# Squares written into an empty slot, weight sums moved around a layer norm, and an idle product in the query projection

## The chip, the cores and the metric

The kernel runs on one core of one Trainium2 chip, as one program. The metric is the device time of one execution in microseconds (us). The core's engines are TensorE (PE in the profile, with its weight loads as PEld), VectorE (DVE), ScalarE (ACT), GpSimd (POOL) and SyncE (SP). SP does no arithmetic here: it issues transfers (DMA), one behind the other in its own order. POOL and ACT issue some transfers too.

## The reference

One layer of an encoder for 512 tokens of width 1024, in float32:

```
n = rms_norm(x);  proj = n @ w_in                  # xa 512 | zu 1024 | zv 1024 | gate_a 1024 | gate_b 1024
ya = s5_branch(xa)                                 # two linear recurrences over the tokens, gelu, a GLU
zv = layer_norm(gelu(zv), ln_g, ln_b)
yb = gelu(zu) * (w_s mixes zv within chunks of 128 tokens, per head, + bias)
h = x + (sigmoid(gate_a) * (ya @ w_proj_a) + sigmoid(gate_b) * (yb @ w_proj_b)) @ w_out
h = h + attention(rms_norm(h) @ w_q, memory keys, memory values) @ w_xo      # 4 heads, 256 memory tokens
h = h + (silu(hn @ w_gate) * (hn @ w_up)) @ w_down                           # hn = rms_norm(h), inner width 2816
out = rms_norm(h)
```

The layer norm of zv is over 1024 columns of a token: the mean is taken off, the squares of what is left are summed, and the row is scaled with the root of their mean.

## The kernel before, in words

**Products.** Every product of float32 matrices is made of three: each operand is split into a high part, rounded to a shorter float, and the low rest (`split`: ACT casts `whi`, line 85, DVE subtracts for `wlo`, line 86), and high times high, high times low and low times high are added up in a PSUM bank. A weight block of 512 KB comes by a DMA that SP issues (`wraw`, three buffers), is split two blocks ahead of its use, and feeds 24 products of 512 columns, or of 256 columns where a product is cut in halves.

**Sums of weights.** w_proj_b, w_q, the gates and w_down are multiplied by a scheme of seven half-size products in place of eight. It needs sums of weight blocks. For w_proj_b and w_q these are made in DRAM: SP copies one block into a scratch tensor (`bsum`, `qsum`; line 272), and POOL adds another onto it by a DMA that accumulates (line 273). `plan_sums` gives each of these jobs a place: the number of the weight block at which SP's copy is issued, and how many blocks later POOL's sum follows. Two of w_proj_b's sums are sums of sums, so SP's copy of such a one waits until POOL's sum has landed.

**The stage of the norm.** From about 90 to 170 us PE does the zv columns and then the gate_a columns of w_in (tiles `pt`, `pf`, 512 columns a product). In between it does small work of the S5 branch: it turns tiles (`pw`, 128 columns), ACT copies them out (`wt`, line 855), and PE multiplies with the copies (`pz`, 64 columns), whose results ACT copies to `zh`. The PSUM banks of `pw` and `pz` are three in turn. The norm of zv runs beside this, for four tiles of 128 tokens (`layer_norm`): ACT takes off the mean (`zt<-zt,nm`, line 996), squares two halves and sums them (`sum_sq`, line 483: the squares themselves, `sq`, are not used, only their sum `ss`), DVE makes the mean (`ms`), POOL the root (`r`, line 1001), and ACT scales (`zt<-zt,r`, line 1002). The tile for the unused squares comes from the pool with the tag `ev`, two buffers. The gate_a tiles that ACT makes (`gas`, line 1035) come from the same pool; SP stores them to DRAM (`gad`, line 1036), and a buffer is free again when its store has landed.

**The query projection.** w_q is multiplied as 14 half-size products of 24 matrix products each, all of 256 columns (`query_product`, line 1098), with the scores of the first heads between them. The operands are parts of `hn` and sums of them (`hse`, `hsd`).

**The units.** The gate and up columns follow the same scheme from about 574 to 794 us (`pf`, `px`, `pv`, `pq`). Once, before the last columns of the gate, `between` issues one idle product (line 1560): weights from the first block of `fn_hi`, 512 columns of its fifth block, into a bank that nobody reads. `fn` and `hn` are tiles of the same two slots at the same addresses.

**What sets the order.** A scheduler orders the instructions of each engine by its own estimate of times; `in_order` pins an instruction to its place in the program. Small side work is handed out by `later` and `tick` between weight blocks.

Of the kernel before, what the change touches and what calls it, by code (L numbers as in the profile page):

```python
# [17 lines left out]
P = 128  # L18
# [34 lines left out]
def hybrid_layer_kernel(  # L53
# [26 lines left out]
    def aux(name, shape=(P, 512)):  # L80
        return pa.tile(list(shape), F32, tag="aux", name=name)
# [175 lines left out]
    def plan_sums(places):  # L257


        jobs = []  # L260
        for w, sums in ((w_proj_b, bsum), (w_q, qsum)):
            for q, first, more in ((5, (0, 0), (0, 1)), (7, (0, 1), (1, 1)), (6, None, (1, 1)), (4, None, (1, 0))):
                for n in range(2):
                    jobs.append((sums[q, n], sums[q + (-1 if q == 6 else 2), n] if first is None else
                                 pair_block(w, *first, n), pair_block(w, *more, n)))
        for q, i, jc, more in ((5, 0, 0, lambda c: down_block(0, 1, c)), (7, 0, 1, lambda c: down_block(1, 1, c)),
                               (6, 1, 1, lambda c: down_sum(5, c)), (4, 1, 0, lambda c: down_sum(6, c))):
            for c in range(CHUNKS):
                jobs.append((down_sum(q, c), down_block(i, jc, c), more(c)))
        assert len(jobs) == len(places)  # L270
        for (dst, src, more), (j, step) in zip(jobs, places):
            plan[j][1].append((0, lambda d=dst, x=src: tc.keep_in_program_order(nc.sync.dma_start(d, x))))
            plan[j + step][1].append((0, lambda d=dst, x=more: nc.gpsimd.dma_start(d, x, accum_op=ALU.add)))  # L273
# [41 lines left out]
    for i in range(4):  # L315
# [4 lines left out]
    plan_down(w_down, lambda q, c: down_tokens[0](q, c), down_plan)  # L320
    plan_units(UNITS, down_plan)

    plan_sums([(j, 3) for j in (5, 8, 11, 13, 15, 17, 20, 22, 25, 28, 32)] + [(51 + 2 * i, 2) for i in range(4)] +
              [(67 + 3 * i, 3) for i in range(3)] + [(85 + 3 * i, 3) for i in range(3)] +
              [(95 + 2 * i, 2) for i in range(3)] + [(122 + 4 * i, 4) for i in range(16)])
    used_w = [0]

    def next_w(*key):
# [122 lines left out]
    def tick(us=5.2):  # L451

        side["now"] += us / 5.2
        run_due()
        side["credit"] = min(side["credit"] + us * side["rate"], us)
        while side["credit"] > 0.0 and side["gen"] is not None:
            try:
                used = next(side["gen"])
            except StopIteration:
                side["gen"] = None  # L460
                return
            if used is None:
                side["credit"] = 0.0
                return
            side["credit"] -= used
# [12 lines left out]
    mhalf = cp.tile([P, 9], F32, name="mhalf")[:, 0:1]  # L478
    nc.vector.memset(mhalf, -0.5)

    def sum_sq(dst, src):
        sq = np_.tile([P, 512], F32, tag="ev", name="sq", bufs=2)
        act = nc.scalar.activation(sq[:, :src.shape[-1]], src, AF.Square, accum_out=dst)
        if pinned[0]:
            in_order(act)
# [501 lines left out]
    tokm(w_in, OFF_V + 512, xn, KD, zv_evac(1))  # L987


    def layer_norm(t):  # L990

        nm, ss, ms, r = (np_.tile([P, 1 + (k == "ss")], F32, tag=k, name=k, bufs=2) for k in ("nm", "ss", "ms", "r"))
        nc.vector.tensor_tensor(nm, zsum[:, t, 0:1], zsum[:, t, 1:2], ALU.add)
        nc.vector.tensor_scalar(nm, nm, -1.0 / GW, None, ALU.mult)
        z = zt[:, t, :]
        nc.scalar.activation(z, z, AF.Identity, bias=nm)
        for i in range(2):
            sum_sq(ss[:, i:i + 1], z[:, HALF[i]])
        nc.vector.tensor_tensor(ms, ss[:, 0:1], ss[:, 1:2], ALU.add)
        nc.vector.tensor_scalar(ms, ms, 1.0 / GW, EPS, ALU.mult, ALU.add)  # L1000
        nc.gpsimd.tensor_tensor(r, ms, mhalf, ALU.pow)
        nc.scalar.activation(z, z, AF.Copy, scale=r)
# [86 lines left out]
    def product(ps, u, q, start, ops):  # L1089

        hi, lo = next_w(u[0], u[1], q)
        for j in range(2):
            cs = slice(j * P, (j + 1) * P)
            for k in range(4):
                a = (hi[:, k, cs], lo[:, k, cs])
                b = (ops[q][0][:, k, :], ops[q][1][:, k, :])
                for i, (x, y) in enumerate(((0, 0), (0, 1), (1, 0))):
                    nc.tensor.matmul(ps[:, j, :], a[x], b[y], start=start and j == k == i == 0,  # L1098
                                     stop=k == 3 and i == 2, skip_group_check=True)
        tick(2.7)  # L1100

    def unit_bank(name):
        return bank(name).rearrange("p (j t) -> p j t", j=2)

    def seed(x):
        v = unit_bank("qv")
        nc.scalar.copy(v, x)
        return v
# [291 lines left out]
    qx, qq_ = unit_bank("qx"), None  # L1400
    query_product(qx, 0, 1, True)
    qv = seed(qx)
    qq_ = unit_bank("qq")
    query_product(qq_, 0, 5, True)
    query_product(qv, 0, 2)
# [149 lines left out]
        feat_block(ps, ws[i], fn, KD, 4, ts, ts is T0)  # L1555
        tick(2.7)

    def between():

        in_order(nc.tensor.matmul(aux("idle"), ops[1][0][:, 0, 0:P], fn_hi[:, 4, :], start=True, stop=True))  # L1560

    gate_part(0, T0)
    begun = unit_start(UNITS[0])
    gate_part(1, T0)
    unit_second(UNITS[0], begun[1])
    between()
    for i in range(2):
        gate_part(i, T1)
    for j in range(2):
# [219 lines left out]
```

## Time and profile before

| | |
|---|---|
| three runs | 902.88, 905.46, 905.97 us (median 905.46) |
| the profiled execution | 903.66 us |
| its span, first to last instruction | 901.9 us |
| mean granted TensorE clock | 0.997 |
| PE busy | 887.9 us (98%) |
| DVE, ACT, POOL busy | 642.8, 484.8, 108.2 us |

The profile is of one execution. An engine's busy time is that of its instructions; an idle time is put down to what ended it. Products of PE overlap: one of 512 columns lasts about 0.40 us and the next one starts about 0.23 us after it, so the distance of starts tells the rate, and the length does not. `x6` behind a row counts merged instructions. SPq and POOLq are issues of transfers.

### The profile page before, as it was taken

The numbers are of one execution on the slowest core, as the hardware profiler recorded it, in microseconds if no ns is written. First come the engines' busy times: TensorE is split into PE (matmuls) and PEld (weight loads), VectorE is DVE, ScalarE is ACT, GpSimd is POOL, SyncE is SP. The second block draws the span as 40 slices with busy tenths as digits, with TensorE's granted clock in tenths as the row PEclk, the third lists the DMA queues.
The fourth block names the chain that finished last, engine by engine and source line by source line (L and its number), as shares of the span: only waits on it lengthen the run. The fifth ranks groups of instructions, "written<-read, shape, count | busy, mean of one in ns | idle before, by whom it ended". The sixth has DMA issues, their size and how long they took to land.

```text
span 901.9 us, 14886 instructions
## 1 busy us (share of the span) xinstructions
PE 887.9 (98%) x5787; PEld 793.5 (88%) x5787; DVE 642.8 (71%) x1048; ACT 484.8 (54%) x714; POOL 108.2 (12%) x165
## 2 busy tenths in 40 slices
PE   9999989999999999999999999999999999999996
PEld 6888878888889998889889978999999999988875
DVE  5696651889857457858856845776778777899875
ACT  5533966344388344447655634655554554665664
POOL 1004410100022201001100101101121111000010
PEclk9999999999999999999999999999999999999999
DMA  7566763566523689854979748429799999356672
GB/s 249 163 156 182 168 164 114 162 140 153 147 89 95 161 264 308 265 157 144 257 239 257 200 117 210 140 50 231 167 263 224 215 226 256 99 161 202 203 234 99
DMA packets 118408, 165.36 MB, mean 183 GB/s; under 512 B 11825, under 2 KB 84161, under 8 KB 118210
## 3 DMA queue, kind: packets, MB, share of 16 engines
q1 hardware_dynamic: 97474, 135.74, 47.2%
q0 software_dynamic: 20576, 28.15, 19.8%
q8 instruction: 45, 0.74, 0.3%
q10 hardware_dynamic: 288, 0.52, 0.2%
q14 instruction: 25, 0.20, 0.1%
HBM read 157.61 MB, written 46.63 MB: 226 GB/s over the span
## 4 chain that ended last, share of the span: by engine, by line
PE 84%; ACT 0%; DVE 0%; issue 0%; POOLq 0%; ACTq 0%
PE pf L356 21%; PE pt L356 12%; PE px L1098 12%; PE dx L356 6%; PE pq L1098 6%; PE dq L356 3%; PE pv L1098 3%; PE bx L1098 3%; PE qx L1098 2%; PE dv L356 2%; PE bq L1098 1%; PE qq L1098 1%; PE qv L1098 1%; PE psc L356 1%; PE po L356 1%; PE ptr L517 1%
## 5 line engine op out<-in xcount | busy, mean ns | idle before, releaser
L86 DVE TENSOR_TENSOR wlo<-wraw,whi 128x1024 fp32r<-128x1024 f32 (+1 forms) x145 | 172.2, 1188 | 100.3 <-ACT whi L85 92.8
L85 ACT CAST whi<-wraw 128x1024 fp32r<-128x1024 f32 (+1 forms) x145 | 148.2, 1024 | 153.5 <-PE pf L356 45.3
L356 PE MATMUL pf<-xn,whi 128*128 128x512 f32 x448 | 140.4, 394 | 0.0
L356 PEld LDWEIGHTS pf<-xn,whi 128*128 128x128 f32 x448 | 83.6, 189 | 16.8
L356 PE MATMUL pf<-xn,wlo 128*128 128x512 f32 x224 | 87.6, 391 | 0.0
L1098 PE MATMUL px<-fn,whi 128*128 128x256 f32 x480 | 83.3, 277 | 0.0
L1098 PEld LDWEIGHTS px<-fn,whi 128*128 128x128 f32 x480 | 72.5, 188 | 0.2
L85 ACT CAST whi<-b 128x1024 fp32r<-128x1024 f32 x40 | 42.2, 1054 | 50.7 <-PE px L1098 27.7
L86 DVE TENSOR_TENSOR wlo<-b,whi 128x1024 fp32r<-128x1024 f32 x40 | 48.9, 1222 | 27.9 <-ACT whi L85 27.9
L1098 PE MATMUL px<-fn,wlo 128*128 128x256 f32 x240 | 66.4, 277 | 0.0
L1098 PE MATMUL pq<-s,whi 128*128 128x256 f32 x320 | 55.0, 276 | 0.0
L356 PE MATMUL dx<-whi,s 128*128 128x512 f32 x170 | 53.6, 391 | 0.4 <-DVE h L1714 0.4
L85 ACT CAST whi<-t 128x1024 fp32r<-128x1024 f32 x30 | 31.6, 1054 | 35.3 <-PE pv L1098 12.4
L86 DVE TENSOR_TENSOR wlo<-t,whi 128x1024 fp32r<-128x1024 f32 x30 | 36.7, 1224 | 19.4 <-ACT whi L85 19.4
L356 PEld LDWEIGHTS pf<-xn,wlo 128*128 128x128 f32 x224 | 42.2, 188 | 8.9
L1098 PEld LDWEIGHTS pq<-s,whi 128*128 128x128 f32 x320 | 48.1, 188 | 0.0
L1098 PEld LDWEIGHTS px<-fn,wlo 128*128 128x128 f32 x240 | 45.1, 188 | 0.0
L1098 PE MATMUL pq<-s,wlo 128*128 128x256 f32 x160 | 44.2, 276 | 0.0
L356 PE MATMUL pt<-whi,xn 128*128 128x512 f32 x128 | 42.9, 406 | 0.1
L356 PEld LDWEIGHTS dx<-whi,s 128*128 128x128 f32 x170 | 31.8, 188 | 7.4 <-issue 0.8
L356 PE MATMUL dx<-wlo,s 128*128 128x512 f32 x85 | 33.1, 391 | 0.0
L273 POOL DMA_DIRECT2D dsum<-in_w_down_dram x12 | 13.3, 1110 | 144.3 <-DMA dsum<-in_w_down_dram 144.3
(456 smaller groups left out, 2308.3 us busy)
## 6 DMA issues: line engine op xcount, KB each, us to landing
wraw<-in_w_in_dram SPq DMA_DIRECT2D x36, 512.0 KB, 4.3
dsum<-in_w_down_dram SPq DMA_DIRECT2D x20, 512.0 KB, 6.0
wraw<-dsum SPq DMA_DIRECT2D x20, 512.0 KB, 4.5
b<-in_w_gate_dram SPq DMA_DIRECT2D x15, 512.0 KB, 5.1
b<-in_w_up_dram SPq DMA_DIRECT2D x15, 512.0 KB, 5.9
wraw<-in_w_down_dram SPq DMA_DIRECT2D x15, 512.0 KB, 4.4
dsum<-in_w_down_dram POOLq DMA_DIRECT2D x10, 512.0 KB, 8.1
dsum<-dsum POOLq DMA_DIRECT2D x10, 512.0 KB, 8.0
```

The lines of the kernel that those rows point to most:

```text
L85: hi = nc.scalar.copy(dst_hi, src)
L86: lo = nc.vector.tensor_tensor(dst_lo, src, dst_hi.bitcast(F32), ALU.subtract)
L273: plan[j + step][1].append((0, lambda d=dst, x=more: nc.gpsimd.dma_start(d, x, accum_op=ALU.add)))
L356: m = nc.tensor.matmul(ps, a[x], b[y], start=start and i == 0, stop=stop and i == 2, skip_group_check=free)
L517: nc.tensor.transpose(ps[:, j, :], src[:, k * P:(k + 1) * P], ident)
L1098: nc.tensor.matmul(ps[:, j, :], a[x], b[y], start=start and j == k == i == 0, stop=k == 3 and i == 2, skip_group_check=True)
```

## The change

Three edits. First, `layer_norm` hands `sum_sq` a place for the squares: slot A, a quarter of which was a token tile of x each, and which is empty between the input norm and `sv`. It has a part for every one of the eight squares, so none waits for a buffer of `ev`. Second, the places of w_proj_b's eight sums: three are at blocks 5, 7 and 9, and the other five at 16 to 24, where before the eight stood at 5, 8, 11, 13, 15, 17, 20 and 22; the first three of w_q go from 25, 28, 32 to 26, 28, 32. Third, the idle product becomes a helper, `idle_product`, with the old use before the gate's last columns and a new one in w_q, behind the first of the 14 products and the copy that follows it.

```
-    plan_sums([(j, 3) for j in (5, 8, 11, 13, 15, 17, 20, 22, 25, 28, 32)] + [(51 + 2 * i, 2) for i in range(4)] +
-              [(67 + 3 * i, 3) for i in range(3)] + [(85 + 3 * i, 3) for i in range(3)] +
-              [(95 + 2 * i, 2) for i in range(3)] + [(122 + 4 * i, 4) for i in range(16)])
+    plan_sums([(5, 3), (7, 3), (9, 2)] + [(j, 3) for j in (16, 18, 20, 22, 24, 26, 28, 32)] +
+              [(51 + 2 * i, 2) for i in range(4)] + [(67 + 3 * i, 3) for i in range(3)] +
+              [(85 + 3 * i, 3) for i in range(3)] + [(95 + 2 * i, 2) for i in range(3)] +
+              [(122 + 4 * i, 4) for i in range(16)])
...
-    def sum_sq(dst, src):
-        sq = np_.tile([P, 512], F32, tag="ev", name="sq", bufs=2)
+    def sum_sq(dst, src, sq=None):
+        if sq is None:
+            sq = np_.tile([P, 512], F32, tag="ev", name="sq", bufs=2)
         act = nc.scalar.activation(sq[:, :src.shape[-1]], src, AF.Square, accum_out=dst)
...
+    squares = slot("A", (P, NT, GW), F32, "squares")
+
     def layer_norm(t):
...
         for i in range(2):
-            sum_sq(ss[:, i:i + 1], z[:, HALF[i]])
+            sum_sq(ss[:, i:i + 1], z[:, HALF[i]], squares[:, t, HALF[i]])
...
+    def idle_product(x, y):
+
+        in_order(nc.tensor.matmul(aux("idle"), x[:, 0, 0:P], y[:, 4, :], start=True, stop=True))
...
     qv = seed(qx)
+    idle_product(hops[1][0], hn_hi)
     qq_ = unit_bank("qq")
...
-    def between():
-
-        in_order(nc.tensor.matmul(aux("idle"), ops[1][0][:, 0, 0:P], fn_hi[:, 4, :], start=True, stop=True))
-
...
-    between()
+    idle_product(ops[1][0], fn_hi)
```

The scheduler answers the new buffers and places with another order in the norm's stage. The line numbers of the changed kernel are 2 to 5 higher.

ACT in the norm's stage before, from the scaling of the first two tiles on. `sq,ss` are the squares with their sums, `gas` the gate tiles:

```order
L1002 ACTIVATE zt<-zt,r 128x1024 x2
...
L855 COPY wt<-pw 128x512 x2
L1035 ACT_TABLE_LOAD
L1035 ACTIVATE gas<-pf_1091 128x512
L85 CAST whi<-wraw 128x1024
L1035 ACTIVATE gas<-pf_1092 128x512
L866 COPY zh<-pz 64x8x64
L867 COPY zh<-pz 64x8x64
L483 ACTIVATE sq,ss<-zt 128x512
L855 COPY wt<-pw 128x512 x2
L483 ACTIVATE sq,ss<-zt 128x512 x3
L855 COPY wt<-pw 128x512
L1002 ACTIVATE zt<-zt,r 128x1024
```

ACT there now:

```order
L485 ACTIVATE squares,ss<-zt 128x512 x2
...
L1006 ACTIVATE zt<-zt,r 128x1024 x2
L1000 ACTIVATE zt<-zt,nm 128x1024
L1006 ACTIVATE zt<-zt,r 128x1024
...
L857 COPY wt<-pw 128x512
L485 ACTIVATE squares,ss<-zt 128x512 x2
L857 COPY wt<-pw 128x512
L1039 ACT_TABLE_LOAD
L1039 ACTIVATE gas<-pf_1093 128x512
L85 CAST whi<-wraw 128x1024
L1039 ACTIVATE gas<-pf_1094 128x512
L1006 ACTIVATE zt<-zt,r 128x1024
```

The squares of the last two tiles, which stood behind the first two gate tiles, stand before them, and so does the third scaling. On PE the `pz` group that uses these two `wt` copies has moved back: 24 products of 512 columns stood between it and the `pw` group before it, now 34.

POOL from the first root of the norm on, before (`bsum_82`, `_79`, `_80`, `_76`, `_75` are sums of w_proj_b; `ss` memsets belong to the S5 branch):

```order
L1001 TENSOR_TENSOR r<-ms,mhalf 128x1
L273 DMA bsum_82<-in_w_proj_b_dram 512x1x256
L1001 TENSOR_TENSOR r<-ms,mhalf 128x1
L273 DMA bsum_79<-in_w_proj_b_dram 512x1x256
L273 DMA bsum_80<-in_w_proj_b_dram 512x1x256
L1001 TENSOR_TENSOR r<-ms,mhalf 128x1 x2
...
L273 DMA bsum_76<-in_w_proj_b_dram 512x1x256
L273 DMA bsum_75<-in_w_proj_b_dram 512x1x256
```

And now:

```order
L1005 TENSOR_TENSOR r<-ms,mhalf 128x1 x4
...
L273 DMA bsum_82<-in_w_proj_b_dram 512x1x256
...
L273 DMA bsum_79<-in_w_proj_b_dram 512x1x256
L273 DMA bsum_75<-in_w_proj_b_dram 512x1x256
L273 DMA bsum_80<-in_w_proj_b_dram 512x1x256
L273 DMA bsum_76<-in_w_proj_b_dram 512x1x256
```

The four roots stand in a row, and the sums that stood between them come behind. Two more (`bsum_78`, `bsum_81`) have moved ahead of the first memsets and stores of the S5 kernels. On SP the copy for `bsum_78` now stands between a weight load and the loads of `rowci`, and the copy `bsum_75<-bsum_79`, which waits for POOL's `bsum_79`, between weight loads and gate stores.

PE in w_q, where the first product (`qx`) ends and the second (`qq`) begins, now; before, the row with `idle` is not there:

```order
L1102 MATMUL qx<-hn,whi 128x256 x2
L1102 MATMUL qx<-hn,wlo 128x256
L1108 MATMUL idle<-hn 128x512
L1102 MATMUL qq<-hse,whi 128x256 x2
L1102 MATMUL qq<-hse,wlo 128x256
```

One product of 512 columns has come in between.

## The prediction

> **What bounds the kernel now.** I read the page first, then the cores, the waits, the timelines of the stage that shows waits, and counts of products in stretches.
>
> ```profile
> PE 887.9 (98%) x5787; PEld 793.5 (88%) x5787; DVE 642.8 (71%) x1048; ACT 484.8 (54%) x714; POOL 108.2 (12%) x165
> PE 84%; ACT 0%; DVE 0%; issue 0%; POOLq 0%; ACTq 0%
> core 0: 901.9 us, clock 0.997
> ```
>
> PE is busy for 98% of the span and is nearly the whole chain that ended last, so a gain needs PE idle time, clock, or the spacing of PE's products. The profiled execution took 903.66 us; its span leaves 1.8 us outside, which the change does not touch. The waits from 90 to 150 us hold most of the idle time that PE has after its start; here PE's two, from its timeline (start, length, and in brackets the idle time before with what ended it), and ACT's two longest:
>
> ```profile
> 127.28 0.66 PE L854 MATMUL pw<-ident,wsx 128*128 128x128 f32 x4 [1.48 <-ACT wt L855]
> 134.57 1.76 PE L861 MATMUL pz<-u,wt 128*128 128x64 f32 x8 [1.87 <-ACT wt L855]
> ...
> ACT sq L483 <- DMA gad<-gas: 4.0, 1, 4.0
> ACT zt L1002 <- POOL r L1001: 2.9, 1, 2.9
> ```
>
> PE waits twice for ACT's copies `wt`. ACT is late for two reasons: a square waits for the store of a gate tile, and a scaling waits for POOL's root `r`. The timelines of ACT, POOL and SP show the places:
>
> ```profile
> 125.90 0.63 ACT L483 ACTIVATE sq<-zt 128x512 f32<-128x512 f32 x1 [4.00 <-DMA gad<-gas]
> 126.64 1.07 ACT L855 COPY wt<-pw 128x512 f32<-128x512 f32 x2
> 132.90 1.15 ACT L1002 ACTIVATE zt<-zt,r 128x1024 f32<-128x1024 f32 x1 [2.87 <-POOL r L1001]
> ...
> 130.82 1.15 POOL L273 DMA_DIRECT2D bsum<-in_w_proj_b_dram  x1 [13.05 <-DVE ms L1000]
> 131.47 2.64 POOL L1001 TENSOR_TENSOR r<-ms,mhalf 128x1 f32<-128x1 f32 x2
> ...
> 118.22 1.77 SPq L1036 DMA_DIRECT2D gad<-gas  x2
> ```
>
> The square shares a pool of two buffers with the gate tiles `gas`, whose stores were issued at 118.22; it starts at 125.90, and the `wt` copies stand behind it in ACT's order. The last roots stand behind a weight sum on POOL. Stretches of equal kind (us, PE busy with its count, clock, DMA) price the rest:
>
> ```profile
> 125.00:127.30 2.30, 0.82 (x7) 0.50 (x5) 0.00 (x0) 1.38 (x4) 0.00 (x0) 1.00 1.07 379
> 132.40:134.60 2.20, 0.33 (x3) 0.03 (x1) 1.27 (x2) 1.70 (x3) 1.71 (x2) 1.00 0.92 89
> 134.60:138.30 3.70, 3.70 (x16) 3.42 (x17) 1.22 (x1) 3.69 (x4) 0.00 (x0) 0.54 0.65 104
> 464.26:498.18 33.92, 33.92 (x291) 1.00 0.88 257
> 583.26:586.79 3.53, 3.53 (x32) 1.00 0.93 242
> 587.39:621.39 34.00, 34.00 (x303) 1.00 0.46 124
> 788.59:794.24 5.65, 5.65 (x49) 1.00 0.19 49
> ```
>
> Right after the second idle the clock is 0.54 over 3.70 us, so 1.70 us of clock is lost. In the last four rows all products but one have 256 columns, and the count holds two or three that run over from before. So w_q's stretch does 288 products at 117.8 ns, and the units' stretch 300 at 113.3 ns: two spacings of the same product, neither with an idle gap. Both last: once begun, each holds for the whole stretch.
>
> **The change part by part.** *Squares into the empty slot.* The four pairs are the same instructions on the same shapes; only the buffer differs, and with it the wait for the gate's store. Removed: PE's 1.48 us behind ACT's 4.00. *Sums around the norm.* Three of w_proj_b's eight sums go ahead of the norm, five behind it, so that POOL has the four roots in a row. Removed: ACT's 2.87 and with it PE's 1.87.
>
> ```profile
> 122.47 0.62 PE L356 MATMUL pf<-xn,whi 128*128 128x512 f32 x2
> 123.15 0.62 PE L356 MATMUL pf<-xn,whi 128*128 128x512 f32 x2
> 117.79 1.89 PE L861 MATMUL pz<-u,wt 128*128 128x64 f32 x16
> 115.21 1.07 ACT L855 COPY wt<-pw 128x512 f32<-128x512 f32 x2
> 109.90 2.18 ACT L1002 ACTIVATE zt<-zt,r 128x1024 f32<-128x1024 f32 x2
> 102.96 0.61 ACT L483 ACTIVATE sq<-zt 128x512 f32<-128x512 f32 x1
> ```
>
> Neither wait can move to the next link for free, since ACT now has more to do early. Ahead of the second `wt` copy that ended at 116.28 stand two more pairs of squares (about 0.61 each, 2.5 together) and one more scaling (half of 2.18): 3.5 us, so it ends near 119.8. PE wants it at 117.79 now; in the new order it does ten more products of 512 columns first (three in 123.15 - 122.47 = 0.68, so 2.3 us), and wants it near 120.1. About 0.3 us of cover is left, and the next two groups of PE stand equally close behind ACT. No row shows ACT this full with that order, so I bound what remains of the waits: nothing, or 2.0 us (ACT late by the 2.5 us of squares at one place, less some cover); I take 0.4, near the low end, because PE was moved by about what ACT gained in work. Upwards, the idle counts begin at the end of a 0.40 us product whose follower would start after 0.23, so each wait may be worth 0.17 more. Clock: 1.70 us, gone if the idle that precedes it is gone.
>
> A rule of the Trainium skill, "TensorE: Matmul & The Clock Gate", section "HAM oscillation — how this bites in real kernels", asks for an idle gap of more than about 3.4 us before the clock falls. Here a gap of 1.87 us, with 1.48 us of idle some 5 us earlier, was followed by the fall: the trace does not agree. Were the fall not due to these gaps, it would stay, which is a rival below.
>
> The three early sums go into 47 to 75 us. The second stands ahead of the loads of `rowci`, which PE turns at 58.09:
>
> ```profile
> 58.09 1.18 PE L652 MATMUL pbc<-ident,rowci 32*128 32x32 f32 x16
> 47.13 0.37 SPq L137 DMA_DIRECT2D wraw<-in_w_in_dram  x1
> 50.71 1.24 SPq L648 DMA_DIRECT2D rowci<-in_s_c_im_dram  x2
> bsum<-in_w_proj_b_dram SPq DMA_DIRECT2D x3, 512.0 KB, 7.3
> rowci<-in_s_c_im_dram SPq DMA_DIRECT2D x2, 128.0 KB, 3.4
> ```
>
> The copy, issued behind the load of 47.13 near 47.6, lands near 54.9 by its row, and `rowci`, 3.4 us from its second issue near 51.3, near 54.7, or, if it must follow the copy in full, at 58.3. So 0 to 0.2 us; I take 0.
>
> *Idle product.* It costs its own place. The same helper stands once before the units' first gate columns:
>
> ```profile
> 586.68 0.28 PE L1098 MATMUL pv<-fn,wlo 128*128 128x256 f32 x1
> 586.79 0.40 PE L1560 MATMUL idle<-fn 128*128 128x512 f32 x1
> 587.03 0.86 PE L356 MATMUL pf<-fn,s 128*128 128x256 f32 x6
> ```
>
> That is 587.03 - 586.79 = 0.24 us. Ahead of it 30 products took 3.53 us (117.7 ns), behind it 300 took 34.00 (113.3). The new one has the same operands by address (both tiles are the same slot), the same kind of product ahead (117.8) and 256-column products behind. If it does the same, 288 products gain 4.4 ns each, 1.28 us; less 0.24 and some 0.03 for the first products: 1.0 us gained. If it does nothing it costs 0.24; these are the ends, and I take the gain.
>
> [...]
>
> Sum: 903.66 - 1.48 - 1.87 - 1.70 + 0.40 - 1.00 = 898.0. The runs of before are 902.88, 905.46 and 905.97, so the profile is 1.8 below their median. I do not add that: what varies between runs may well be these waits on transfers. The upper end of the range holds it.
>
> **The rivals.** (1) *The idle product does not switch the spacing.* For it: the twelve products of 512 columns that end at 788.59 leave the 48 behind them at 117.7. Against: those take weights and columns from different tiles, and 586.79 is the closer match. 903.66 - 4.65 + 0.24 = 899.3. (2) *The clock falls all the same.* For it: the clock's window need not begin with the gap. Against: the fall begins at the very end of the second gap, and the rows before and behind it have a clock of 1.00. 898.0 + 1.7 = 899.7. (3) *ACT becomes the bound of the norm's stage*, with the squares on top of a full engine:
>
> ```profile
> 100.00:122.00 22.00, 22.00 (x135) 19.44 (x134) 15.06 (x19) 21.67 (x28) 5.12 (x5) 1.00 0.59 130
> ```
>
> It is busy for 21.67 of 22 us. Against: it then stands idle for 4 us, so the work fits. With the whole 2.0 us left: 899.6; if such a wait brings the clock down too, 901.3. (4) *Spacing is a matter of chance in time, not of operands*, so that any shift undoes it: w_q stays slow and pays 0.24, and the units' 1,700 products from 587 to 780 fall back by 4.4 ns, 7.5 us: 899.3 + 7.5 = 906.8, slower. It decides where the units' stretch begins. Against: the rows around 587 hang on what PE does just before, which is unchanged. (5) *SP stands still.* Its copies for the last sums wait for POOL's sums to land, and weight loads and gate stores queue behind them:
>
> ```profile
> bsum<-in_w_proj_b_dram POOLq DMA_DIRECT2D x7, 512.0 KB, 6.6
> bsum<-bsum SPq DMA_DIRECT2D x4, 512.0 KB, 5.3
> SPq L137 <- DVE wlo L86: 48.5, 8, 14.4
> ```
>
> Copy and sum take 11.9 us. Weight loads already wait 48.5 us for free buffers, and three blocks of 24 products (5.4 us each) lie ahead, so a hold hurts from about 16.3 - 3.7 (a load's landing) = 12.6 us on. Were POOL itself 10 us late there, two holds would cost some 9 each: 916, slower. Against: no cast of ACT waits for a load in these rows.
>
> **How the numbers follow.** Forecast 0.57 (897 to 899.5 by its own bounds), (1) 0.17, (2) 0.07, (3) 0.11, (4) 0.05, (5) 0.03. A measurement of this kernel tells 0.3% (2.7 us) from no change. Forecast to (3) lie 3.5 us or more under the median, of which I leave 0.06 for runs near the edge: faster 0.86; same 0.09, from that and half of (4) and (5) mild; slower 0.05. The range 895.4 to 902.0 takes in (1) to (3), both 0.17 above, and most of the runs' own spread.
>
> **What would show it.** Right: no PE wait for `wt` between 90 and 150, no square behind a gate's store, four roots in a row on POOL, clock 1.00 there; an idle product of some 0.24 us at about 459, and some 300 products in the 34 us behind it. Wrong: a wait of PE for ACT near 120 to 128; 288 products behind the idle one; a gap at `pbc` near 58; a cast that waits for a load near 165 to 200; the units at 117.8.

## The result, and the profile after

The changed kernel takes 898.43 us (median of 16 runs, 896.11 to 903.09), the kernel before 902.93 us (16 runs, the three shown above among them). The ratio is 0.9948 with a 95% interval of 0.9932 to 0.9963: 4.7 us faster, between 3.3 and 6.1. The forecast was 898.0 us, the range 895.4 to 902.0. One run of a later kernel (e10_act), 1271.64 us at a granted clock of 0.65, is in the slow state and stays out of that kernel's ratio.

The profiled execution of the changed kernel took 901.19 us, with a span of 899.4: it is the second longest of the sixteen, and that has to be kept in mind when the two profiles are compared. The page of the changed kernel:

```profile
span 899.4 us, 14887 instructions
PE 885.8 (98%) x5788; PEld 791.0 (88%) x5788; DVE 642.8 (71%) x1048; ACT 484.8 (54%) x714; POOL 106.8 (12%) x165
```

Its stretches of the norm's stage (us, then busy time and count of PE, PEld, DVE, ACT, POOL, then the granted clock, DMA share, GB/s), at the same times as those shown of before:

```profile
100.00:122.00 22.00, 22.00 (x128) 19.18 (x127) 14.03 (x22) 21.87 (x35) 2.62 (x3) 1.00 0.21 62
125.00:127.30 2.30, 2.30 (x12) 1.91 (x11) 2.23 (x3) 2.27 (x4) 0.00 (x0) 1.00 0.77 244
132.40:134.60 2.20, 2.20 (x22) 2.20 (x22) 1.67 (x2) 1.78 (x3) 0.00 (x0) 1.00 0.49 170
134.60:138.30 3.70, 3.70 (x20) 3.07 (x19) 0.00 (x0) 3.48 (x5) 0.00 (x0) 1.00 0.20 73
```

Where PE was busy for 0.82 of 2.30 us and for 0.33 of 2.20, it is now busy throughout, and the clock behind is 1.00 where it was 0.54. ACT does more in the same 22 us (21.87 busy, 35 instructions for 28). The places themselves, from the timelines of POOL, ACT and PE:

```profile
97.08 0.56 POOL L1005 TENSOR_TENSOR r<-ms,mhalf 128x1 f32<-128x1 f32 x1
120.80 0.55 POOL L1005 TENSOR_TENSOR r<-ms,mhalf 128x1 f32<-128x1 f32 x1 [8.04 <-ACT wt L857]
120.11 0.58 ACT L857 COPY wt<-pw 128x512 f32<-128x512 f32 x1
121.00 1.89 PE L863 MATMUL pz<-u,wt 128*128 128x64 f32 x16
```

The first and the last of the four roots wait for no weight sum. The copy `wt` that the prediction worried about ends at 120.69, and PE wants it at 121.00: 0.31 us of cover, where 0.3 was worked out.

How much that is worth shows best from two fixed points of PE that lie on either side of the stage: the first product `pbc` and the first `psv`. Of before, then of the changed kernel:

```profile
31.25 1.94 PE L652 MATMUL pbc<-ident,rowbr 32*128 32x32 f32 x16
...
171.32 0.94 PE L1051 MATMUL psv<-wsx,zt 128*128 128x128 f32 x7
```

```profile
32.19 1.94 PE L654 MATMUL pbc<-ident,rowbr 32*128 32x32 f32 x16
...
166.82 3.73 PE L1055 MATMUL psv<-wsx,zt 128*128 128x128 f32 x32
```

From 140.07 us to 134.63: 5.44 us less. The same can be done for the rest: from `psv` to w_q's first product 290.10 before and 292.06 after, from there to the first product `po` behind the scores (w_q's stage) 45.81 and 46.18. So this execution gained 5.44 in the norm's stage, and lost 0.94 ahead of it, 1.96 behind it and 0.37 in w_q. The idle product's stage, which was to gain 1.0, came out longer. Its rows:

```profile
461.58 0.28 PE L1102 MATMUL qx<-hn,wlo 128*128 128x256 f32 x1
461.70 0.40 PE L1108 MATMUL idle<-hn 128*128 128x512 f32 x1
461.94 0.40 PE L1102 MATMUL qq<-hse,whi 128*128 128x256 f32 x2
```

and the stretches ahead of it and behind it:

```profile
458.88:461.70 2.82, 2.82 (x25) 2.82 (x24) 2.35 (x4) 1.71 (x3) 0.00 (x0) 1.00 0.66 224
462.29:488.00 25.71, 25.71 (x229) 25.70 (x228) 12.92 (x14) 12.14 (x16) 2.27 (x2) 1.00 0.78 231
```

The idle product does what it was to do: 24 products in 2.82 us ahead of it (117.5 ns, one runs over from before) and some 227 in 25.71 behind it (113.3 ns). It cost 0.24 us. Yet the 1.0 us did not arrive in this execution: two distances of `qq` near 489 us were together 0.3 us too long, PE waited 0.23 us for `prob` near 496 us, and behind that wait the products ran at 117.8 ns to the end of the stage, where in every other profile they end it at 113.3. Some lines of PE's list of waits over the span:

```profile
PE pt L357 <- DVE wlo L86: 1.3, 2, 0.8
PE pt L357 <- ACT whi L85: 0.8, 2, 0.5
PE ppt L1387 <- DVE prob L1378: 0.2, 1, 0.2
```

Whether these waits belong to the change or to this execution is what the experiments had to say first.

### The profile page after: what moved, and what is told of

Same layout as the page of the kernel before. It is cut to its first block, busy times and chain, and to the rows that moved or that the text cites. A ratio compares the mean times of both kernels' runs of the same rounds, so it can differ in the third digit from the quotient of the medians.

```text
span 899.4 us, 14887 instructions
## 1 busy us (share of the span) xinstructions
PE 885.8 (98%) x5788; PEld 791.0 (88%) x5788; DVE 642.8 (71%) x1048; ACT 484.8 (54%) x714; POOL 106.8 (12%) x165
## 4 chain that ended last, share of the span: by engine, by line
PE 94%; DMA 3%; ACT 1%; DVE 1%; SPq 1%; issue 0%; POOL 0%; POOLq 0%; ACTq 0%
PE pf L357 26%; PE pt L357 16%; PE px L1102 12%; PE dx L357 6%; PE pq L1102 6%; PE dq L357 3%; PE pv L1102 3%; PE qx L1102 2%; PE bx L1102 2%; PE dv L357 2%; PE pz L863 2%; PE pk L806 2%; PE qq L1102 1%; PE bq L1102 1%; DMA slab<-in_s_log_step_dram 1%; PE psc L357 1%
```

## The experiments

The theory after the result (T1): the norm's part is the whole gain, and the 1.2 us of w_q's spacing are given back in waits. Against it stand the prediction's own sum (T2, 1.0 us net for the idle product) and chance (T3, the spacing in w_q has nothing to do with the idle product). The first four kernels take the change apart.

**Without the new idle product (e1_norm).**

```
-    idle_product(hops[1][0], hn_hi)
```

> The change without the new idle product in w_q: squares in slot A and the moved sums are kept. Theory T1 (the norm's part is the whole gain; the idle product switches the spacing, but w_q's attention steps give its 1.2 us back in waits and spacing): no PE wait for wt from 90 to 150 us, clock 1.00 there, PE's starts behind the norm 5.4 us earlier than in the kernel before (1.65 + 2.04 between starts, 1.70 of clock); time as the changed kernel, within 0.3 us of it, about 4.5 below before. Theory T2 (the prediction: the idle product is worth 1.0 net): about 1.0 us above the changed kernel, 3.5 below before. Theory T3 (w_q's first stretch at 113.3 ns in the changed kernel came from the shift in time and not from the idle product): here too 113.3 ns from the second product of w_q on, and 0.24 us below the changed kernel.

Measured: 898.23 us (10 runs), ratio 0.9953 (0.9935 to 0.9971). From `pbc` to `psv` 134.62 us, as in the changed kernel; w_q at 117.8 ns from its first product on, its stage 45.81 us as before. T1's number, and T3 falls: without the product, this execution has no switch.

**The idle product alone (e2_idle).** The kernel before, with

```
     qv = seed(qx)
+    idle_product(hops[1][0], hn_hi)
```

> The kernel before with the idle product in w_q alone. The norm's stage stays as before: PE idle near 127 and 134 us and clock near 0.5 behind it. T1: 256-column products of w_q at 117.8 ns ahead of the idle product and at 113.3 ns behind it, for some 260 products (1.2 us earlier by the end of that stretch), and most of it given back before the heads' last products, by waits for prob or by later products that fall to 117.8 ns: time within 0.3 us of before. T2: 1.0 us below before, the start of w_o's first product (pt behind the heads) 1.0 us earlier against w_q's first. T3: no switch, 0.24 us above before.

Measured: 903.13 us (12 runs), ratio 1.0004 (0.9985 to 1.0023). No gain in time. But its trace does not bear T1 out: the spacing switches behind the idle product, and w_q's stage is 44.96 us, 0.85 shorter than 45.81, with nearly nothing given back. So the single execution shows a gain of 0.85 and the times of twelve show none, with a standard error of some 0.6 us, so that they do not exclude it. One more thing is seen here: the norm's stage took 139.09 us, not 140.07, though its program is that of before.

**The squares alone (e3_squares).** The changed kernel with the old table of places and without the new idle product.

> Squares in slot A alone, with the old places of w_proj_b's sums and no new idle product. Two weight sums still stand between the roots on POOL, but the scheduler now puts all squares and the third and fourth scalings ahead of the second gate tile. If each PE gap has its own cause as the prediction reads it: the first gap (1.65 us between starts) is gone, and what is left is at most one gap of 0 to 2 us where ACT scales behind a sum on POOL. Clock: if the fall needs the gap of 1.87 us or one like it, it goes with that gap and stays with it; if it comes at this place anyway (a rival), 1.7 us of clock loss stays with no gap ahead of it. Time between 1.6 us (gap left, clock lost) and 5.4 us (neither) below before; I expect the latter, since the scalings that waited now have a gate tile and a cast less ahead.

Measured: 903.04 us (10 runs), ratio 1.0004 (0.9987 to 1.0021). The stage is cured (134.63 us from `pbc` to `psv`, no gap, no fall of the clock), and the time is that of before. From 90 to 150 us ACT waits neither for a store nor for a root, although two weight sums still stand between POOL's roots: the last root starts at 119.00 us there, where the kernel before has its last two from 131.47 us on. So the squares' edit alone takes away both waits. What was gained is lost between `psv` and w_q: 295.59 us, where the others have 289.4 to 292.1. PE's waits from 150 to 460 us, of which the kernel before has none:

```profile
PE pf L356 <- ACT ya_hi L85: 1.1, 1, 1.1
PE bq L1101 <- ACT s L85: 0.8, 1, 0.8
PE pt L356 <- DVE wlo L86: 0.5, 1, 0.5
PE bq L1101 <- DVE s L86: 0.3, 1, 0.3
PE bx L1101 <- ACT u L1119: 0.2, 1, 0.2
```

The scheduler had answered the new buffers with another order not only in the norm's stage but also in w_proj_b, where PE now does a group of `bq` products earlier and waits for their sums, and at `ya_hi`. These waits are 2.9 us of the 5.5; the rest was not taken apart. My expectation of 5.4 us was right for the stage and wrong for the kernel.

**The moved sums alone (e4_sums).** The changed kernel with the squares back in the pool of the gate tiles, and without the new idle product:

```
-            sum_sq(ss[:, i:i + 1], z[:, HALF[i]], squares[:, t, HALF[i]])
+            sum_sq(ss[:, i:i + 1], z[:, HALF[i]])
```

> The moved sums alone, with the squares still in the pool of the gate tiles and no new idle product. The four roots stand in a row, so no scaling waits for POOL and the gap of 1.87 us is gone (2.04 between starts). Two pairs of squares still stand behind the gate tiles, so a square waits some 4 us for the store of one, and PE some 1.5 us behind it. Clock: if it takes both gaps, or the longer one, the clock stays at 1.00 and the time is 3.7 us below before; if one gap of 1.5 us is enough, the clock falls some microseconds behind it and the time is 2.0 below before.

Measured: 899.94 us (10 runs), ratio 0.9965 (0.9946 to 0.9984). From `pbc` to `psv` 136.58 us, 3.49 less than before (expected 3.7). The square still waits for a gate's store, but 1.5 us and not 4.0: the store is issued at 118.26, where it was 118.22, and the square starts at 121.15, where it was 125.90. The sums that were moved away had also been in this store's way, it seems: from 90 to 150 us the transfers took 0.35 of the DMA engines here, and 0.65 in the kernel before (r3_before). ACT's and PE's waits there:

```profile
ACT sq L485 <- DMA gad<-gas: 1.5, 1, 1.5
ACT zt L1004 <- POOL r L1003: 1.0, 2, 0.8
...
PE pw L856 <- ACT zh L869: 1.0, 1, 1.0
PE pz L863 <- ACT wt L857: 0.5, 1, 0.5
```

Two gaps of 1.0 and 0.5 us, and the clock stays at 1.00.

Two of these kernels, e3_squares and e4_sums, had entered w_q at 113.3 ns without an idle product there. That made a new theory, T4: the spacing at that place is set anew in every execution, and the idle product gains only where it finds 117.8. The next two kernels are repetitions, to part the kernels by more runs and to see a second execution of each.

**The changed kernel again (r1_after).** No edit.

> The changed kernel once more, beside the same kernel without its idle product in w_q, to part the two by more runs and to see a second profiled execution. The kernels tried so far without that idle product entered w_q at 117.8 ns in two executions and at 113.3 ns in two others, so a new theory T4: without it the spacing there is set by chance (where PE's last wait ahead of w_q falls), and the idle product gains only where chance has set 117.8. T4: w_q's first product at either spacing, 113.3 ns behind the idle product in any case; time within 0.5 us of the kernel without it (gain 1.0 in about half the executions, loss 0.24 in the others: 0.4 below on average). T2 (the prediction): 1.0 us below the kernel without it.

**The change without the new idle product again (r2_norm).** No edit against e1_norm.

> The change without the idle product in w_q once more, unchanged from the first time, to see a second profiled execution of the same instructions. T4 (the spacing is set anew in each execution): w_q may run at 113.3 ns here, where it ran at 117.8 the first time, with the last wait of PE ahead of w_q at another product. The rival (the spacing belongs to the program, its operands and order): w_q at 117.8 ns again, all 311 products of it. Time as before, 898.2 within 0.7.

Measured: 896.50 us (5 runs, ratio 0.9931, 0.9918 to 0.9943) with the idle product and 897.79 (5 runs, 0.9942, 0.9930 to 0.9954) without. In these runs, taken side by side, the means are 897.01 and 898.03: 1.0 us less with the idle product, with a standard error of 0.5. The earlier runs, taken at different times, say 0.3 more (898.68 in 16 runs, 898.38 in 10; standard error 0.55), and all runs thrown together 0.0 (898.28 in 21 runs, 898.26 in 15; 0.45). The times therefore do not decide between T2's 1.0 and T4's 0.4; the traces have to. The stretches of w_q, of r1_after and then of r2_norm:

```profile
458.73:491.00 32.27, 32.27 (x287) 32.27 (x286) 19.46 (x28) 18.69 (x30) 3.35 (x3) 1.00 0.90 262
```

```profile
455.73:492.40 36.67, 36.67 (x313) 36.66 (x312) 22.31 (x31) 20.67 (x32) 3.40 (x3) 1.00 0.85 252
```

285 products in 32.27 us (113.3 ns) against 311 in 36.67 (117.8). The stage took 44.80 us in r1_after and 45.81 in r2_norm: in this execution the idle product gained 1.01 us, as forecast, and no wait took it back. So T1 falls as well: the waits in the first profile of the changed kernel were that execution's. r2_norm came to w_q at 117.8 again, which fits T4 and its rival alike; that the same order can come to it at 113.3 is shown by e6_idle256 below, whose PE has the same order up to that place.

**No idle product at all (e5_no_idle).** Against e1_norm:

```
-    idle_product(ops[1][0], fn_hi)
```

> The change without any idle product: neither the new one in w_q nor the old one ahead of the gate's last columns. If that product is what sets the spacing: the gate's last columns and the units go on at 117.8 ns as the products ahead of it, 1,701 products of 256 columns at 4.5 ns more, 7.6 us less its own 0.24: 905.6, 7.3 above the kernel with it. If the spacing of the units is set by something else (chance, or the products that follow): 113.3 ns there, and 0.2 us below, 898.0.

**The old idle product with 256 columns (e6_idle256).** Against e1_norm:

```
-        in_order(nc.tensor.matmul(aux("idle"), x[:, 0, 0:P], y[:, 4, :], start=True, stop=True))
+        in_order(nc.tensor.matmul(aux("idle")[:, 0:256], x[:, 0, 0:P], y[:, 4, 0:256], start=True, stop=True))
```

> The change without the idle product in w_q, and with the old idle product ahead of the gate's last columns cut from 512 to 256 columns, same weights and place. If what switches the spacing is one product of another length between products of 256 columns: no switch here, the units at 117.8 ns, 7.5 us above the kernel with 512 columns, 905.7. If any added product shifts the spacing (by its operands, or by its time alone): 113.3 ns behind it, and 0.1 us below, 898.1.

Measured: 905.12 us (10 runs, ratio 1.0017, 1.0003 to 1.0032) and 905.31 us (10 runs, 1.0029, 1.0013 to 1.0045), where 905.6 and 905.7 were expected. The units, first of e5_no_idle, then of e6_idle256, and in the second also w_q:

```profile
582.00:616.00 34.00, 34.00 (x291) 34.00 (x290) 24.48 (x24) 17.54 (x20) 1.68 (x2) 1.00 0.45 123
```

```profile
456.20:491.00 34.80, 34.80 (x310) 34.80 (x308) 21.21 (x29) 20.48 (x32) 3.02 (x3) 1.00 0.88 258
576.46:610.00 33.54, 33.54 (x287) 33.54 (x286) 23.45 (x23) 17.50 (x21) 2.07 (x2) 1.00 0.44 118
```

288 products in 34.00 us and 284 in 33.54 are 118 ns each: without the 512 columns the units stay at the wider spacing for all of their 1,701 products, and from the first `px` to the first `dx` they take 213.54 and 213.65 us, where every other kernel takes 206.21 (but for e7_pauses below, which has pauses there). The idle product is the cause of the narrower spacing, and it is its length that counts: the same weights and the same place with 256 columns do nothing. The first row of e6_idle256 shows w_q at 113.3 ns (307 products in 34.80) with no idle product there.

**Which gaps make the clock fall (e7_pauses).** Against e1_norm, ahead of each unit from the second on, with the units' products held in their written order:

```
+    def pause(n):
+        g = aux("pause")
+        in_order(nc.tensor.matmul(g, ops[1][0][:, 0, 0:P], fn_hi[:, 4, :], start=True, stop=True))
+        for _ in range(n):
+            in_order(nc.scalar.copy(g, g))
+        in_order(nc.tensor.matmul(g, ops[1][0][:, 0, 0:P], fn_hi[:, 4, :], start=True, stop=True))
...
+        if i:
+            pause(1 + i % 3)
```

> The change without the new idle product, with nine pauses of PE put into the units, to see which gaps make the clock fall: ahead of each unit from the second on an idle product of 512 columns, one, two or three copies of ACT in its bank (some 0.5 us each, behind what ACT is at), and the same idle product again, which has to wait for them; the units' products are held in their written order. Expected gaps 1 to 3 us, nine of them, so some 20 to 25 us more in all. So far the clock fell behind gaps of 1.86 and 1.87 us and not behind 1.48, 1.09 and 1.01, and each record of the granted clock lasts a multiple of 3.413 us. Theory T5: the clock of a stretch of 3.413 us follows from how long PE stood idle in the stretch before it on that grid, with the bound between 1.48 and 1.86 us (43 to 54% of it): gaps over 1.9 us that lie within one stretch make it fall, gaps under 1.5 do not, and one of 2 to 3 us that is cut by a grid line may pass. Rival (only a gap longer than a whole stretch, or no gap at all, makes it fall): no fall, or falls with no gap ahead.

Measured: 935.26 us in one run, nine gaps of 1.31 to 3.05 us, and four falls of the clock ahead of the kernel's end, each 3.413 us long. All starts of falls lie on one grid of 3.413 us. Stretches of that grid, always one with a gap and the next one, for six of the nine gaps:

```profile
618.19:621.60 3.41, 1.41 (x11) 1.36 (x12) 2.46 (x3) 1.83 (x4) 0.00 (x0) 1.00 0.99 165
621.60:625.01 3.41, 3.41 (x19) 3.41 (x18) 0.00 (x0) 0.22 (x1) 0.00 (x0) 0.50 0.41 138
...
686.45:689.86 3.41, 1.67 (x14) 1.35 (x12) 3.41 (x5) 2.39 (x4) 0.87 (x1) 1.00 1.11 239
689.86:693.27 3.41, 3.24 (x26) 3.20 (x27) 2.81 (x3) 0.12 (x1) 0.00 (x0) 1.00 1.06 198
710.34:713.76 3.42, 0.37 (x2) 0.16 (x2) 3.08 (x4) 3.14 (x5) 0.86 (x1) 1.00 1.21 170
713.76:717.17 3.41, 3.41 (x16) 3.32 (x17) 0.00 (x0) 0.00 (x0) 0.00 (x0) 0.50 0.94 220
754.72:758.13 3.41, 2.08 (x17) 1.76 (x15) 3.41 (x4) 2.42 (x4) 0.82 (x2) 1.00 1.15 206
758.13:761.54 3.41, 2.29 (x18) 2.25 (x19) 1.55 (x2) 1.04 (x2) 0.00 (x0) 1.00 0.98 166
778.62:782.03 3.41, 1.15 (x9) 0.83 (x8) 3.41 (x5) 2.46 (x4) 0.81 (x1) 1.00 1.19 202
782.03:785.44 3.41, 3.15 (x13) 3.06 (x14) 2.29 (x3) 0.21 (x1) 0.00 (x0) 0.50 1.06 205
802.50:805.92 3.42, 1.71 (x14) 1.39 (x12) 3.42 (x5) 2.44 (x4) 0.00 (x0) 1.00 0.00 0
805.92:809.33 3.41, 3.27 (x26) 3.23 (x27) 1.17 (x2) 0.08 (x1) 0.00 (x0) 1.00 0.23 77
```

The clock falls behind a stretch in which PE was busy for 1.41 us or less, and does not behind 1.67 or more. The gap of 2.45 us near 757 is cut by the grid line at 758.13 into 1.33 and 1.12, and passes; the one of 2.52 near 781 lies for 2.26 us in one stretch, and does not. The kernel before and e2_idle, with the same order there, fit, each with the grid from its own fall:

```profile
131.42:134.84 3.42, 1.55 (x8) 0.98 (x7) 2.25 (x2) 1.94 (x3) 2.69 (x3) 1.00 0.67 71
134.84:138.25 3.41, 3.41 (x15) 3.14 (x15) 1.22 (x1) 3.40 (x4) 0.00 (x0) 0.50 0.62 98
```

```profile
130.69:134.11 3.42, 1.56 (x14) 1.51 (x14) 1.65 (x2) 3.19 (x4) 1.45 (x2) 1.00 0.94 144
134.11:137.52 3.41, 3.41 (x10) 2.65 (x9) 0.64 (x1) 3.37 (x4) 0.00 (x0) 0.50 0.45 141
```

So the bound lies between 1.56 and 1.67 us busy of 3.413, and no gap of the nine speaks against T5; the rival falls.

**More work for ACT (e10_act).** Against e1_norm:

```
+            if t == 3:
+                sum_sq(ss[:, i:i + 1], z[:, HALF[i]], squares[:, t, HALF[i]])
```

> The change without the new idle product, with both squares of the last token tile done twice (0.61 us each, 1.22 us more for ACT, between the two wt copies of the first pair that follows; nothing else moves). It measures the cover that the prediction gave as 0.3 us. In the changed kernel the second copy wt ends at 120.69 and PE's pz that wants it starts at 121.00. If the cover is 0.3: PE waits some 0.9 us for wt near 120 us, no clock loss (below 1.5 us), and the time is 0.9 above the kernel without the extra squares, 899.0. If ACT has more slack than that (rival): no wait, 898.2. If ACT is the bound from there on (the prediction's rival 3): 1.2 us or more, in several waits.

Measured: 898.49 us (10 runs), ratio 0.9955 (0.9938 to 0.9973). I had put the squares of the last tile in the wrong place: they stand behind the second `wt` copy and the first gate tile, so the cover at 121 us was not tried. What was tried is the next place, where PE's third group comes:

```profile
127.27 0.39 PE L357 MATMUL pf<-xn,wlo 128*128 128x512 f32 x1
127.75 1.27 PE L856 MATMUL pw<-ident,wsx 128*128 128x128 f32 x8
```

PE starts `pw` 0.48 us behind the product ahead of it, not 0.23, and the `pz` behind it another 0.24 us late, and the stage takes 135.19 us from `pbc` to `psv`, 0.56 more than 134.63. Of 1.22 us of added work on ACT 0.56 come through to PE, so the cover is some 0.7 us there. ACT is near to being the bound of this stage, and is not.

**Only the five late sums moved (e9_late5).** Against e1_norm:

```
-    plan_sums([(5, 3), (7, 3), (9, 2)] + [(j, 3) for j in (16, 18, 20, 22, 24, 26, 28, 32)] +
+    plan_sums([(5, 3), (8, 3), (11, 3)] + [(j, 3) for j in (16, 18, 20, 22, 24, 26, 28, 32)] +
```

> The change without the new idle product and with the first three sums of w_proj_b back at their old places (blocks 5, 8 and 11); only the five late ones are moved. On the engines only POOL changes: two sums stand behind the kernel of the S5 branch instead of ahead of it. The prediction gave the early moves no price and no gain, so: the roots still in a row, no PE wait for wt, time as the kernel with all eight moved, 898.2 within 0.7. If the early moves matter (POOL's two sums now stand nearer to the norm): a root late, and a wait of PE of up to 2 us, 900.

Measured: 898.53 us (10 runs), ratio 0.9957 (0.9938 to 0.9975); PE has no wait from 90 to 150 us. The early moves are worth nothing that can be measured, as priced. (From `pbc` to `psv` this execution took 136.21 us, of which 1.6 are a fall of the clock at 33.88, with no gap of PE ahead of it. PE was busy for the whole stretch of the grid before, 30.46 to 33.88, but for only 1.4 us of it with products of all 128 rows; the rest were 17 small products of 32 rows and 32 columns, `plam` and `pbc`. In the other profiles the stretches with such products hold at least 1.54 us of full ones, and no fall follows. So products this small seem not to count in full for the clock; no run tests it by itself.)

**The kernel before again (r3_before).** No edit.

> The kernel before in a second profiled execution. T4 and T5: the two gaps of PE in the norm's stage are there again, of a similar length (they hang on the landing of a store and on a sum on POOL); the clock falls behind the second one only if it lies within one stretch of the clock's grid; w_q and the products of w_proj_b near 310 to 335 us may run at 113.3 ns this time. The rival, that all of it belongs to the program: the same gaps, the same fall and the same spacings as in the first profile.

Measured: 899.98 us in the profiled run, 3.68 less than the first profile of the same program. PE's two longest gaps and ACT's two waits in the norm's stage (a third gap of PE, behind `zh`, is 0.4 us long):

```profile
PE pw L854 <- ACT wt L855: 1.5, 1, 1.5
PE pz L861 <- ACT wt L855: 0.7, 1, 0.7
...
ACT sq L483 <- DMA gad<-gas: 4.0, 1, 4.0
ACT zt L1002 <- POOL r L1001: 1.7, 1, 1.7
```

The first is as it was. The second is 0.7 us and not 1.87, since the weight sum ahead of the last roots was issued at 129.99 and not at 130.82, and the roots behind it took 2.22 us and not 2.64; and the clock does not fall. The stage took 137.93 us. w_q ran at 113.3 ns from its first products on, and so did the products of w_proj_b near 320 us: T4 and T5 hold, and the rival, that all of it belongs to the program, falls.

The three stages side by side, in us, each from one profile, without e7_pauses (w_q: with or without its idle product, and the spacing on coming in):

| kernel | median | `pbc` to `psv` | `psv` to w_q | w_q's stage |
|---|---|---|---|---|
| before, first and second profile | 902.93 | 140.07, 137.93 | 290.10, 289.56 | 45.81 (117.8), 44.47 (113.3) |
| changed, first and second profile | 898.43, 896.50 | 134.63, 134.63 | 292.06, 289.39 | 46.18, 44.80 (with idle, 117.8 both) |
| without new idle product, twice | 898.23, 897.79 | 134.62, 134.63 | 290.02, 289.83 | 45.81, 45.81 (117.8 both) |
| idle product alone | 903.13 | 139.09 | 289.62 | 44.96 (with idle, 117.8) |
| squares alone | 903.04 | 134.63 | 295.59 | 44.46 (113.3) |
| sums alone | 899.94 | 136.58 | 289.66 | 44.47 (113.3) |
| no idle product at all | 905.12 | 134.63 | 291.08 | 45.81 (117.8) |
| old idle product of 256 columns | 905.31 | 134.62 | 289.86 | 44.46 (113.3) |
| late sums only | 898.53 | 136.21 | 289.42 | 44.47 (113.3) |
| extra squares | 898.49 | 135.19 | 289.74 | 45.81 (117.8) |

No kernel tried is faster than the changed one by more than can be measured.

## Why the prediction was right, and where it was not

The time was right (898.0 for 898.43), and so was the sum of the larger term, that of the norm's stage, though the roots' wait went with another edit than the one named. The smaller term, the idle product's, holds only in executions that come to w_q at the wider spacing. That the whole came out so close is in part luck: a base that was 0.7 us too high stood against a gain that was 1.2 too large.

- **The squares' wait and the roots' wait (-1.48 and -1.87).** Both waits of ACT are gone, and with them PE's, as forecast. But the second was put down to the wrong edit: in e3_squares the squares alone take away both, with two weight sums still between the roots, and in e4_sums the moved sums alone leave 1.5 us of the first and 1.0 us of the second. What the moved sums do beside the squares was no term of the prediction: without them the stretch from `psv` to w_q takes 295.59 us, with them 290.02 and 289.83 (e1_norm, r2_norm). By the distance of starts the two waits of PE were worth 1.65 and 2.04, the 0.17 each that I had named and not taken.
- **What remains of the waits (+0.40).** Nothing remained. The working behind it (copy at 119.8, PE at 120.1) met the trace to 0.1 us, once the 0.94 us by which that execution began late is taken off; then it should have said zero.
- **The clock (-1.70).** Right: it stays at 1.00 where the gap is gone. With these three the stage gained 5.44 us against the profile that was shown, where 4.65 was forecast. But that profile had the long second gap. Three executions of the old order lost 5.44, 3.30 and 4.46 us against 134.63, so 4.4 on average, and the kernel with this part alone is 4.6 and 5.4 us faster in its medians, each against the runs of before that were taken beside it. The term came out near the mean of a thing that varies, from a profile at its upper end.
- **A rule on the clock.** I set the Trainium skill's gap of more than 3.4 us against a fall behind 1.87 us, and took the trace's side. The runs decide for the trace: what counts is how long PE is idle within one stretch of a grid of 3.413 us, and some 1.9 us there are enough. The same page of the Trainium skill, "TensorE: Matmul & The Clock Gate", section "What's actually happening", speaks of a free-running window of 3413 ns; with that the nine gaps of the pauses agree, and only the limit of 3.4 us for a gap does not.
- **The idle product (-1.00).** This is the step that held only in part. The size is right where w_q is entered at 117.8 ns: 1.01 us in r1_after, 0.85 in e2_idle (the first profile of the changed kernel lost it again to late products, a wait and the wider spacing behind it). But "288 products at 117.8" was taken from one profile as if it were a property of the program. Of eleven executions without the new idle product six entered at 117.8 and five at 113.3, where it has nothing to gain and would cost its own 0.24 us (not tried, since all three executions with it came in at 117.8). That is an estimate of some 0.4 us on average over these kernels. In the nine profiles with the changed kernel's order of PE up to w_q, seven came in at 117.8 and two at 113.3, which makes it some 0.7 for this kernel. The times show between 1.0 less and 0.3 more, with standard errors of 0.5 to 0.6, so how much of the 4.5 us is the idle product's stays open.
- **The base (903.66, and "I do not add that").** Of three runs shown the median was 905.46, of sixteen it is 902.93. Taking the profile's own time was the better choice by luck of the sample: the sum of -5.65 from 903.66 was 1.2 too much for the medians (-4.5), and the base 0.7 too high.
- **The rivals.** (1) falls: in all three executions the product switches the spacing. (2) falls: no gap, no fall there in any profile with both edits. (3) falls for the order as it is, with 0.3 us of cover at 121 and 0.7 at 128. (4) is half right: the spacing is a matter of chance at w_q and w_proj_b, but not in the units, where the idle product sets it in all twelve profiles that have it at full length, and where leaving it out makes the way from `px` to `dx` 7.3 us longer, against the 7.5 worked out. (5) falls: the one wait of SP for a weight sum is 1.2 us long, and PE has no wait from 150 to 300 us behind it:

```profile
SPq L272 <- DMA bsum<-in_w_proj_b_dram: 1.2, 1, 1.2
```

- **Not foreseen.** That the squares alone would gain nothing (e3_squares) was no rival of mine. The two parts of the norm's edit do not add: the squares alone are 0.2 us slower, the sums alone 2.9 faster, both together 4.6. The squares alone cure the stage, and their kernel loses the gain behind it, in another order of PE; what in that order costs the part of the 5.5 us that is no wait stays open.

## What to carry to other kernels

Before a spacing or a gap in one profile is priced as a term, ask whether it belongs to the program or to that execution: a second profile of the unchanged kernel is cheap, and here it would have shown that the idle product's term hangs on how the execution comes to w_q. Where two edits each have a wait to their name, try each alone: here one edit removed both waits, and the other was needed for a later stage. Read a stage by the distance between two fixed products on either side of it, since that distance repeats to 0.01 us where nothing varies, and shows a change that the whole time hides. And when an edit frees a buffer under a scheduler, look at the order of all later stages, not only at the stage that was cured.

## What the runs showed of the hardware

- **Two spacings of one stream.** Products of 256 columns with a weight load each ran at 113.3 or 117.8 ns, for some 1,700 in a row, with the clock at 1.00 in both. One product of 512 columns between them switches from the wider to the narrower (12 times of 12 ahead of the units, 3 of 3 in w_q), one of 256 columns does not (once). The narrower one can be lost again: in the first profile of the changed kernel 117.8 ns came back behind a wait of 0.23 us.
- **What sets it on coming in.** Ahead of w_q stand products of 512 columns, whose distances go 226, 229, 232 ns in turn. In all nine profiles that entered w_q at 117.8 ns the last of these distances was 226 or 227; in the five that entered at 113.3 it was 230 to 236. Which of the three comes last does not follow from the product at which PE last waited: the last distance over 245 ns stands 21 or 57 products ahead of w_q in all fourteen, and both spacings occur behind each. What sets the phase, and why it has this effect, stays open.
- **The clock's grid.** The granted clock changes on a grid of 3.413 us whose phase differs between executions. In e7_pauses and in the norm's stage it halved for one stretch behind a stretch with PE busy for 1.56 us or less, and did not behind 1.67 or more, so a gap of 1.9 to 2.5 us cost 1.7 us where 1.86 us or more of it lay in one stretch, and nothing where a grid line left at most 1.75 in one. Four falls come behind stretches with PE busy for 2.5 to 3.4 us: the one at 33.88 us in e9_late5 and those at 7.5 to 7.8 us in e2_idle, e5_no_idle and e10_act. Only 0.7 to 1.4 us of these stretches are products of all 128 rows; the rest are products of one row (`pg`) or of 32 rows.
